# Fixed 256-byte offsets for the split weights of a decoder trunk, and another order of three-product sums

## Chip, cores and metric

The kernel runs on one core of a Trainium2 chip. The metric is the device time of one execution in microseconds; the median of several runs counts.

## What is computed

One layer of a hybrid decoder trunk on 256 tokens of width 1024, in float32. Every large product is an activation (256 tokens) times a weight:

```
proj = rmsnorm(x) @ w_in                      # 1024 x 3088, shared by three head groups
x = x + concat(shortconv, moba attention, gated linear attention) @ w_out
h = rmsnorm(x);  m = rmsnorm(mem)             # mem: 256 tokens
x = x + cross_attention(h @ wq, m @ wkv) @ wo # 4 heads of 64
h = rmsnorm(x)
u = causal_dwconv(h @ w_up)                   # 1024 x 5504, width 3
x = x + (silu(u[:, :2752]) * u[:, 2752:]) @ w_down
return rmsnorm(x)
```

## The kernel before

**Three products for one.** TensorE multiplies float32 data in the type float32r, to which float32 values are rounded. So each operand is split in two: `high` is the value rounded to float32r (a copy on ScalarE, line 159), `low` is the rest (a subtraction on VectorE, line 165). A product is summed in PSUM from (high, high), (high, low) and (low, high); in the code the pairs are (0, 0), (0, 1), (1, 0), the stationary operand first. A tile of 128 output features over 1024 inputs takes 8 blocks of inputs times 3 = 24 matmuls of 256 columns.

**Weights stream in.** `_stream_order` lists all pieces of weights in the order of use, at most 1024 columns each. `emit_load` brings a piece into one of six raw buffers by a DMA on SP's queue; `emit_split` makes its `high` and `low` in two pools of four buffers each (`hp`); `piece` hands them out and keeps six loads and two splits ahead.

**Who is stationary.** In the feature products the weights are the stationary operand and the activations (`xg`, `y`, `xo`, `memg`, `hn2`) move, 256 columns each: `first` (line 300, six output tiles at once), `feature_tile` (line 218: tiles `in`, `xk`, `xq`, `up`), `products` (line 207: `out`), `wo_part` (773) and the first pair of `up` (867). In the token products the activations are stationary and the weights move: `gla` (455, 272 columns), `mv` (471, 512 columns), `memv` (731, 256 columns) and `down` (905 and 909, 512 columns, 260 matmuls at the end of the kernel, with the hidden values `hid` stationary).

**Where the parts lie.** A buffer of `hp` has 1024 + 32 elements, 4224 bytes, which is 16.5 times 256. So the four buffers of a pool begin at 0, 128, 0 and 128 bytes modulo 256 in turn. A weight that moves begins at the buffer's start, a stationary one 16 elements (64 bytes) behind it:

```
at0 = 0 if key[0] in MOVING else ASIDE
hi, lo = (hp.tile([P, SLOT + 32], F32R, tag=tag, ...)[:, at0:at0 + n] for tag in ("high", "low"))
```

**Order.** The instructions of each engine are put in order by the tile framework; VectorE's order in the loop over `first` and some splits are pinned by hand. `feature_tile` lists all (0, 0) products, then all (0, 1), then all (1, 0); blocks in `late` come behind the others.

Of the kernel before, what the change touches and what calls it, by code (L numbers as in the profile page):

```python
# [10 lines left out]
F32 = mybir.dt.float32  # L11
BF16 = mybir.dt.bfloat16
F32R = mybir.dt.float32r
# [6 lines left out]
P = 128  # L20
T = 256
# [21 lines left out]
EARLY, STATS, TURNED = 3, (1, 0), 3  # L43
# [6 lines left out]
SLOT = 1024  # L50


ASIDE = 16
MOVING = ("gla", "mv", "memv", "down", "dtail")

PADDED = 32

# [18 lines left out]
def _width(key):  # L76
    return {"first": 768, "gla": 544}.get(key[0], 1024)
# [3 lines left out]
def trunk(ctx: ExitStack, tc: tile.TileContext, xT, x_rows, w_stream, params, gate, final, out):  # L81
    nc = tc.nc
    pe, act, dve, pool, sp = nc.tensor, nc.scalar, nc.vector, nc.gpsimd, nc.sync

    cp = ctx.enter_context(tc.tile_pool(name="cp", bufs=1))
    rp = ctx.enter_context(tc.tile_pool(name="rp", bufs=RAW))
    hp = ctx.enter_context(tc.tile_pool(name="hp", bufs=PARTS))
# [6 lines left out]
    def ps(name):  # L94
        banks["turn"] += 1
        return pp.tile([P, 512], F32, tag=banks["tags"][banks["turn"] % len(banks["tags"])], name=name)

    def t1(name):
        return t1p.tile([P, T], F32, tag="t1", name=name)

    def t2(name):
        return t2p.tile([P, 2, T], F32, tag="t2", name=name)

    def small(name, n=2):
        return smp.tile([P, 4], F32, tag="sm", name=name)[:, :n]
# [4 lines left out]
    raw, parts = {}, {}  # L110
    spare = {}
# [22 lines left out]
    def emit_split(pin=False):  # L134
        i = state["split"]
        state["split"] += 1
        key = order[i]
        if key[0] == "mem":
            return
        n = _width(key)  # L140
        t = raw[key]
        if key in SPARE:
            tag = SPARE[key]
            if key[-1] == 0:
                spare[tag] = cp.tile([P, 4 * SLOT + 32], F32R, tag=tag, name="spare_" + tag)
            view = lambda c: spare[tag][:, ASIDE + c * SLOT:ASIDE + (c + 1) * SLOT]
            hi, lo = view(2 * key[-1]), view(2 * key[-1] + 1)
        elif key[0] == "dtail":
            hi = cp.tile([P, n], F32R, name="h_dtail")
            lo = lo_dtail  # L150
        else:
            at0 = 0 if key[0] in MOVING else ASIDE
            hi, lo = (hp.tile([P, SLOT + 32], F32R, tag=tag, name=tag[0] + "_" + "_".join(map(str, key)))[:, at0:at0 + n]
                      for tag in ("high", "low"))
        if i == 0:
            act.copy(hi[:, :384], t[:, :384])
            dve.tensor_copy(hi[:, 384:], t[:, 384:n])
        else:
            c = act.copy(hi, t[:, :n])  # L159
            if pin:  # L160
                tc.keep_in_program_order(c)
        if key[0] == "dtail":
            c = dve.tensor_sub(lo[:TAIL], t[:TAIL, :n], hi[:TAIL])
        else:
            c = dve.tensor_sub(lo, t[:, :n], hi)  # L165
        if pin:
            tc.keep_in_program_order(c)
        parts[key] = (hi, lo)

    def piece(*key):  # L170

        i = place[key]
        while state["load"] < min(len(order), i + RAW):
            emit_load()
        while state["split"] < min(len(order), i + 1 + AHEAD, state["until"]):
            emit_split()
        return raw[key] if key[0] == "mem" else parts[key]

    def blocks(w, n):
        return [a.rearrange("p (k n) -> p k n", n=n) for a in w]  # L180
# [9 lines left out]
    def gained(dst, i, src, g, on=act):  # L190

        if on is act:
            act.activation(dst[0][:, i, :], src, AF.Copy, scale=g)  # L193
        else:
            dve.tensor_scalar(dst[0][:, i, :], src, g, None, op0=ALU.mult)
        dve.scalar_tensor_tensor(dst[1][:, i, :], src, g, dst[0][:, i, :], op0=ALU.mult, op1=ALU.subtract)

    def pair(t, n):

        return t[:, 0:n, :], t[:, n:2 * n, :]  # L200
# [5 lines left out]
        for n, (s, m) in enumerate(todo):  # L206
            pe.matmul(dst, s, m, start=(n == 0), stop=(n == len(todo) - 1))  # L207

    def feature_tile(dst, w, src, late=(), at=None, call=None):
        wb = blocks(w, P)  # L210
        ks = [k for k in range(KT) if k not in late]
        term = lambda k: ([a[:, k, :] for a in wb], [a[:, k, :] for a in src])
        todo = [(k, a, b) for g in (ks, late) for a, b in ((0, 0), (0, 1), (1, 0)) for k in g]
        for n, (k, a, b) in enumerate(todo):
            if n == at:
                call()
            s, m = term(k)
            pe.matmul(dst, s[a], m[b], start=(n == 0), stop=(n == len(todo) - 1))  # L218
# [29 lines left out]
    at = cp.tile([P, 4, T], F32, tag="at", name="at")  # L248
# [22 lines left out]
                       channel_multiplier=-1)  # L271
    pool.memset(tri[0:64, 64:128], 0.0)

    rel = cp.tile([P, 384], F32, name="rel")
    pool.iota(rel[:, 0:P], pattern=[[-1, P]], base=0, channel_multiplier=1, allow_small_or_imprecise_dtypes=True)
    pool.iota(rel[:, P:384], pattern=[[-1, T]], base=P, channel_multiplier=1, allow_small_or_imprecise_dtypes=True)
    pool.affine_select(out=rel[:, 0:P], in_=rel[:, 0:P], pattern=[[-1, P]], compare_op=ALU.is_ge, fill=MASKED,
# [15 lines left out]
    with tc.manual_schedule(engines={mybir.EngineType.DVE}):  # L293
        for k in range(KT):
            state["until"] = place[("first", k)] + 1
            gained(xg, k, x[:, k, :], xt[:, k:k + 1], dve)
            w = piece("first", k)
# [23 lines left out]
    def root_of(sums, name):  # L321

        rt = smp.tile([P, 2], F32, tag=name + "_rt", bufs=1, name=name + "_rt")
        act.activation(rt, sums, AF.Ln, bias=eps, scale=1.0 / D)
        act.activation(rt, rt, AF.Exp, scale=-0.5)
        diags = t1(name + "_diag")
        for j in range(2):
            dve.tensor_scalar(diags[:, j * P:(j + 1) * P], ident, rt[:, j:j + 1], float(D), op0=ALU.mult, op1=ALU.mult)
        return rt, diags
# [120 lines left out]
    for i in range(4):  # L450
        w = blocks(piece("gla", i), 272)
# [23 lines left out]
    q = ps("lrT")  # L475
# [72 lines left out]
    for h in range(4):  # L548
        q = ps(f"a{h}")
# [4 lines left out]
    q = ps("keT")  # L554
# [12 lines left out]
    for n, dst in ((0, ue[:, 0:P]), (2, ue[:, P:T]), (1, uo[:, 0:P])):  # L567
        a = 64 * (n % 2)
# [18 lines left out]
    for j in range(2):  # L587
        for h in range(4):
            a = 64 * (h % 2)
# [23 lines left out]
    for c in range(2):  # L613
        g, s = t1(f"g{c}"), t1(f"sg{c}")
# [20 lines left out]
    for i in range(2):  # L635
        q = ps(f"xk{i}")
# [17 lines left out]
    for o in range(KT):  # L654
        q = ps(f"out{o}")
# [46 lines left out]
    for i in range(2):  # L702
        q = ps(f"xq{i}")
# [39 lines left out]
    for c in range(2):  # L743
        o = ps(f"xo{c}")
        for m in range(2):
            for h in (2 * c, 2 * c + 1):
                a = 64 * (h % 2)
# [5 lines left out]
    xg2 = pair(xgt, KT)  # L753
# [5 lines left out]
    def residual_turned(n):  # L759
        for t in range(2):  # L760
            q = acc[t, n] = pp.tile([P, 512], F32, tag="sd", name=f"dn{t}_{n}")
            for k in range(4):
                pe.matmul(q[:, k * P:(k + 1) * P], x2[:, 4 * n + k, t * P:(t + 1) * P], ident, start=(k == 0), stop=(k == 3),
                          is_transpose=True)
            act.activation(t2(f"x2_sq{t}_{n}").rearrange("p a b -> p (a b)"), q, AF.Square,
                           accum_out=sum2[:, 2 * n + t:2 * n + t + 1])
# [30 lines left out]
    hn2 = pair(hnt, KT)  # L797
# [29 lines left out]
    def freed(j, src):  # L827

        s2 = t2(f"us{j}")
        for t in range(2):  # L830
            dve.tensor_mul(s2[:, t, :], src[t], r2)
        return j, [s2[:, 0, :], s2[:, 1, :]]
# [16 lines left out]
    for j in range(NPAIR + 1):  # L849
        tail = j == NPAIR  # L850
        src = []
        for t in range(1 if tail else 2):
            w = piece("uptail") if tail else piece("up", j, t)
            if j > 0:
                q = ps(f"up{j}_{t}")
                src.append(q[:, :T])
                stats = (j, t) == STATS
                feature_tile(q[:, :T], w, xg2 if j < EARLY else hn2, (), 12 if stats else None, second_root)
            elif t == 1:

                q = ps("up0")
                src = [q[:, :T], q[:, T:]]
                for k in range(KT):
                    for tt in range(2):
                        wb = blocks(piece("up", 0, tt), P)
                        for a, b in ((0, 0), (0, 1), (1, 0)):
                            pe.matmul(src[tt], wb[a][:, k, :], xg2[b][:, k, :], start=(k + a + b + tt == 0),
                                      stop=(k == KT - 1 and a == 1 and tt == 1))
                    if k == TURNED:
                        residual_turned(1)  # L870
                tot2 = small("x2_tot")
                dve.tensor_add(tot2, sum2[:, 0:2], sum2[:, 2:4])
                _, diags2 = root_of(tot2, "x2")
                tc.keep_in_program_order(act.preload_act_table_set("silu_and_others"))
            if (j, t) == STATS:
                early.append(freed(*ready.pop()))
                for k in range(0, KT, 2):
                    f = t2(f"hn{k}")
                    dve.tensor_mul(f, x2[:, k:k + 2, :], r2.unsqueeze(1).to_broadcast([P, 2, T]))
                    for i in range(2):  # L880
                        gained(hn2, k + i, f[:, i, :], gain(PG_FFN, k + i))
                activate(*early.pop())
        ready.append((j, src))
        if j >= STATS[0]:
            for args in ready:
                activate(*(freed(*args) if j < EARLY else args))
            ready = []
# [153 lines left out]
```

## Time and profile before

| | |
|---|---|
| median of 3 runs | 331.56 us (331.46 to 331.89) |
| the profiled execution | 332.42 us |
| its span, first to last instruction | 330.7 us |
| TensorE busy | 321.2 us, 97% |
| VectorE busy | 257.3 us, 78% |
| ScalarE busy | 211.0 us, 64% |

The span is what the rows below divide up. Matmuls are pipelined: each lasts longer in the record (some 276 ns for 256 columns) than the time from its start to the next one's start. The rate of a stream of matmuls is therefore read from starts.

### The profile page before, as it was taken

To read this page: it belongs to the slowest core of one execution; us is meant where nothing else is said; L and a number is where in the kernel's file an instruction comes from. 1 tells how busy PE (TensorE), PEld (TensorE's weight loads), DVE (VectorE), ACT (ScalarE), POOL (GpSimd) and SP (SyncE) were. 2 spreads that over 40 slices of the span, in tenths; PEclk is the share of its full clock that TensorE was granted. 3 is DMA by queue.
4 is the path that set the end of the run, shared out by engine and by line. 5 is a ranking of instruction groups with operands and counts; after the bars stand their busy time and mean duration, and the time that the engine had idled before them with its cause. 6 is when DMAs were issued, how large, how long until landed. Compare 5 with 4: busy or idle time off the path is not lost.

```text
span 330.7 us, 6398 instructions
## 1 busy us (share of the span) xinstructions
PE 321.2 (97%) x2462; PEld 296.4 (90%) x2462; DVE 257.3 (78%) x498; ACT 211.0 (64%) x390; POOL 2.7 (1%) x16
## 2 busy tenths in 40 slices
PE   7999999999999999999999999999999999999992
PEld 4899878899999998899999999999999988888881
DVE  6879978797998858588999999898979974444421
ACT  2583999485676647487977676666667753363322
POOL 3000000000000000000000000000000000000000
PEclk9999999999999999999999999999999999999999
DMA  7979862754368643207067877666557766551003
GB/s 216 405 290 311 270 225 93 254 168 154 108 192 298 208 154 127 66 0 251 5 195 231 271 215 229 197 191 192 191 193 203 235 187 208 191 190 65 0 0 127
DMA packets 17888, 60.38 MB, mean 183 GB/s; under 512 B 1969, under 2 KB 2626, under 8 KB 17858
## 3 DMA queue, kind: packets, MB, share of 16 engines
q1 hardware_dynamic: 17426, 59.26, 54.5%
q10 hardware_dynamic: 432, 0.72, 0.6%
q8 instruction: 19, 0.31, 0.4%
q14 instruction: 11, 0.09, 0.1%
HBM read 58.93 MB, written 1.05 MB: 181 GB/s over the span
## 4 chain that ended last, share of the span: by engine, by line
PE 86%; ACT 6%; DVE 4%; DMA 2%; SPq 1%; issue 0%; ACTq 0%
PE up L218 30%; PE dn L905 18%; PE in L218 10%; PE out L207 7%; PE v L471 3%; DMA w_first<-in_w_stream_dram 2%; PE gv L455 2%; PE xv L731 2%; PE wo L773 2%; PE xq L218 2%; PE xk L218 2%; ACT h_up L159 2%; PE first L300 1%; DVE l_first L165 1%; ACT hn L193 1%; PE et L398 1%
## 5 line engine op out<-in xcount | busy, mean ns | idle before, releaser
L218 PE MATMUL up<-hn,h_up 128*128 128x256 f32 x576 | 71.2, 276 | 0.0
L218 PEld LDWEIGHTS up<-hn,h_up 128*128 128x128 f32 x576 | 68.0, 188 | 0.0
L159 ACT CAST h_up<-w_up 128x1024 fp32r<-128x1024 f32 x40 | 41.7, 1049 | 18.9 <-PE up L218 18.9
L905 PE MATMUL dn<-h_down,hid 128*128 128x512 f32 x168 | 52.8, 392 | 0.0
L165 DVE TENSOR_TENSOR l_up<-w_up,h_up 128x1024 fp32r<-128x1024 f32 x40 | 48.7, 1222 | 4.5 <-ACT h_up L159 3.6
L165 DVE TENSOR_TENSOR l_down<-w_down,h_down 128x1024 fp32r<-128x1024 f32 x21 | 25.7, 1224 | 24.5 <-ACT h_down L159 24.5
L218 PE MATMUL up<-hn,l_up 128*128 128x256 f32 x288 | 38.6, 276 | 0.3 <-DVE l_up L165 0.3
L159 ACT CAST h_down<-w_down 128x1024 fp32r<-128x1024 f32 x21 | 22.0, 1047 | 25.7 <-PE dn L905 25.2
L905 PEld LDWEIGHTS dn<-h_down,hid 128*128 128x128 f32 x168 | 31.5, 188 | 7.1
L218 PEld LDWEIGHTS up<-hn,l_up 128*128 128x128 f32 x288 | 35.3, 188 | 0.5 <-DVE l_up L165 0.5
L804 DVE SCALAR_TENSOR_TENSOR u<-up,par,u 128x255 f32<-128x255 f32 (+1 forms) x74 | 34.5, 477 | 0.5
L905 PE MATMUL dn<-l_down,hid 128*128 128x512 f32 x84 | 32.9, 392 | 0.0
L218 PE MATMUL in<-xg,h_in 128*128 128x256 f32 x192 | 25.1, 283 | 0.0
L218 PEld LDWEIGHTS in<-xg,h_in 128*128 128x128 f32 x192 | 23.1, 188 | 0.7 <-issue 0.5
L802 ACT ACTIVATE u<-up,par 128x256 f32<-128x256 f32 x37 | 20.4, 554 | 0.0
L905 PEld LDWEIGHTS dn<-l_down,hid 128*128 128x128 f32 x84 | 15.8, 188 | 3.6
L207 PE MATMUL out<-y,h_out 128*128 128x256 f32 x128 | 16.0, 277 | 0.0
L165 DVE TENSOR_TENSOR l_in<-w_in,h_in 128x1024 fp32r<-128x1024 f32 x12 | 14.5, 1218 | 1.0 <-ACT h_in L159 1.0
L207 PEld LDWEIGHTS out<-y,h_out 128*128 128x128 f32 x128 | 15.3, 188 | 0.0
L159 ACT CAST h_in<-w_in 128x1024 fp32r<-128x1024 f32 x12 | 12.5, 1046 | 4.1 <-issue 2.7
L300 PEld LDWEIGHTS first<-xg,h_first 128*128 128x128 f32 x96 | 11.6, 188 | 3.1 <-ACT h_first L159 2.1
L300 PE MATMUL first<-xg,h_first 128*128 128x256 f32 x96 | 12.8, 282 | 1.6 <-ACT h_first L159 1.4
(270 smaller groups left out, 542.7 us busy)
## 6 DMA issues: line engine op xcount, KB each, us to landing
w_up<-in_w_stream_dram SPq DMA_DIRECT2D x42, 512.0 KB, 4.3
w_down<-in_w_stream_dram SPq DMA_DIRECT2D x21, 512.0 KB, 3.6
w_in<-in_w_stream_dram SPq DMA_DIRECT2D x12, 512.0 KB, 4.6
w_out<-in_w_stream_dram SPq DMA_DIRECT2D x8, 512.0 KB, 3.3
w_first<-in_w_stream_dram SPq DMA_DIRECT2D x7, 384.0 KB, 8.7
w_mv<-in_w_stream_dram SPq DMA_DIRECT2D x4, 512.0 KB, 5.7
w_gla<-in_w_stream_dram SPq DMA_DIRECT2D x4, 272.0 KB, 4.7
xtok<-in_x_rows_dram SPq DMA_DIRECT2D x1, 1024.0 KB, 10.4
```

The lines of the kernel that those rows point to most:

```text
L159: c = act.copy(hi, t[:, :n])
L165: c = dve.tensor_sub(lo, t[:, :n], hi)
L207: pe.matmul(dst, s, m, start=(n == 0), stop=(n == len(todo) - 1))
L218: pe.matmul(dst, s[a], m[b], start=(n == 0), stop=(n == len(todo) - 1))
L300: pe.matmul(fps[i][:, :T], w[a][:, i * P:(i + 1) * P], xg[b][:, k, :], start=(k == 0 and (a, b) == (0, 0)), stop=(k == KT - 1 and a == 1))
L455: pe.matmul(gps[j][:, :272], xg[a][:, 2 * i + k, j * P:(j + 1) * P], w[b][:, k, :], start=(i == 0 and k == 0 and (a, b) == (0, 0)), stop=( ...
L471: pe.matmul(vps[j], xg[a][:, 2 * i + k, j * P:(j + 1) * P], w[b][:, k, :], start=(i == 0 and k == 0 and (a, b) == (0, 0)), stop=(i == 3 an ...
L731: pe.matmul(vps[j][:, :T], mg[a][:, 4 * i + k, j * P:(j + 1) * P], w[b][:, k, :], start=(i == 0 and k == 0 and (a, b) == (0, 0)), stop=(i ...
L773: pe.matmul(wps[o][:, :T], wb[a][:, 2 * (o % 4) + k, :], xo[b][:, k, :], start=(k == 0 and a + b == 0), stop=(k == 1 and a == 1))
L802: act.activation(v, src, AF.Identity, bias=fb(t), scale=fw(t, 2))
L804: dve.scalar_tensor_tensor(v[:, s:], src[:, :T - s], fw(t, 2 - s), v[:, s:], op0=ALU.mult, op1=ALU.add)
L905: pe.matmul(q, hid[i](k)[:, cols], w[j], start=False, stop=(k == NPAIR - 1 and i == 1), skip_group_check=True)
```

## The change

Each buffer of `hp` becomes 1024 + 64 elements, 4352 bytes or 17 times 256, so all buffers begin at 0 modulo 256. Moving weights stay at the start; of stationary weights `high` lies at 64 and `low` at 192. The weights `memv` leave the list of those that lie at the start. The two larger spare tiles, which hold the parts of `wo` and of the first `up` pair, get 32 elements between their quarters. Two paddings (32 elements at `rel` and at the spare tile `parts`) shift what lies behind them by 128 bytes. The scratch that is kept for DMA descriptors shrinks to 4096 bytes and makes room.

The offsets modulo 256, added up from the tiles' sizes in the order of their allocation, in bytes:

| operands | weight before (high / low) | weight after | other operand before | after |
|---|---|---|---|---|
| `first`, `in`, `xq`, `out`: weight stationary | 64 or 192, both alike | 64 / 192 | 128 | 128 |
| `xk`, `up` from the fourth pair on: weight stationary | 64 or 192, both alike | 64 / 192 | 0 | 0 |
| `up`, pairs two and three: weight stationary | 64 or 192, both alike | 64 / 192 | 128 | 128 |
| `up`, first pair: weight stationary | 192 / 192 | 192 / 64 | 128 | 128 |
| `wo`: weight stationary | 192 / 192 | 192 / 64 | 128 | 0 |
| `mv`, `gla`, `down`: weight moves | 0 or 128, both alike | 0 / 0 | 128 | 128 |
| `memv`: weight moves | 0 or 128, both alike | 64 / 192 | 0 | 0 |

In `feature_tile` the second and third products now alternate: after the eight (0, 0) come (0, 1) and (1, 0) of one block, then of the next. So high and low weights take turns as the stationary operand. That holds for 16 tiles (twelve `in`, two `xk`, two `xq`); the `up` tiles keep the old order with `turns=False`. No instruction is added or taken away, and no transfer changes.

```diff
--- before.py
+++ after.py
@@ -51,7 +51,7 @@
 
 
 ASIDE = 16
-MOVING = ("gla", "mv", "memv", "down", "dtail")
+MOVING = ("gla", "mv", "down", "dtail")
 
 PADDED = 32
 
@@ -142,16 +142,16 @@
         if key in SPARE:
             tag = SPARE[key]
             if key[-1] == 0:
-                spare[tag] = cp.tile([P, 4 * SLOT + 32], F32R, tag=tag, name="spare_" + tag)
-            view = lambda c: spare[tag][:, ASIDE + c * SLOT:ASIDE + (c + 1) * SLOT]
+                spare[tag] = cp.tile([P, 4 * (SLOT + 32) + (32 if tag == "parts" else 0)], F32R, tag=tag, name="spare_" + tag)
+            view = lambda c: spare[tag][:, ASIDE + c * (SLOT + 32):ASIDE + c * (SLOT + 32) + SLOT]
             hi, lo = view(2 * key[-1]), view(2 * key[-1] + 1)
         elif key[0] == "dtail":
             hi = cp.tile([P, n], F32R, name="h_dtail")
             lo = lo_dtail
         else:
-            at0 = 0 if key[0] in MOVING else ASIDE
-            hi, lo = (hp.tile([P, SLOT + 32], F32R, tag=tag, name=tag[0] + "_" + "_".join(map(str, key)))[:, at0:at0 + n]
-                      for tag in ("high", "low"))
+            high, low = (0, 0) if key[0] in MOVING else (ASIDE, 3 * ASIDE)
+            hi, lo = (hp.tile([P, SLOT + 64], F32R, tag=tag, name=tag[0] + "_" + "_".join(map(str, key)))[:, at0:at0 + n]
+                      for tag, at0 in (("high", high), ("low", low)))
         if i == 0:
             act.copy(hi[:, :384], t[:, :384])
             dve.tensor_copy(hi[:, 384:], t[:, 384:n])
@@ -206,11 +206,17 @@
         for n, (s, m) in enumerate(todo):
             pe.matmul(dst, s, m, start=(n == 0), stop=(n == len(todo) - 1))
 
-    def feature_tile(dst, w, src, late=(), at=None, call=None):
+    def feature_tile(dst, w, src, late=(), at=None, call=None, turns=True):
         wb = blocks(w, P)
         ks = [k for k in range(KT) if k not in late]
         term = lambda k: ([a[:, k, :] for a in wb], [a[:, k, :] for a in src])
-        todo = [(k, a, b) for g in (ks, late) for a, b in ((0, 0), (0, 1), (1, 0)) for k in g]
+        todo = []
+        for g in (ks, late):
+            todo += [(k, 0, 0) for k in g]
+            if turns:
+                todo += [(k, a, 1 - a) for k in g for a in (0, 1)]
+            else:
+                todo += [(k, a, 1 - a) for a in (0, 1) for k in g]
         for n, (k, a, b) in enumerate(todo):
             if n == at:
                 call()
@@ -271,7 +277,7 @@
                        channel_multiplier=-1)
     pool.memset(tri[0:64, 64:128], 0.0)
 
-    rel = cp.tile([P, 384], F32, name="rel")
+    rel = cp.tile([P, 384 + 32], F32, name="rel")[:, :384]
     pool.iota(rel[:, 0:P], pattern=[[-1, P]], base=0, channel_multiplier=1, allow_small_or_imprecise_dtypes=True)
     pool.iota(rel[:, P:384], pattern=[[-1, T]], base=P, channel_multiplier=1, allow_small_or_imprecise_dtypes=True)
     pool.affine_select(out=rel[:, 0:P], in_=rel[:, 0:P], pattern=[[-1, P]], compare_op=ALU.is_ge, fill=MASKED,
@@ -855,7 +861,7 @@
                 q = ps(f"up{j}_{t}")
                 src.append(q[:, :T])
                 stats = (j, t) == STATS
-                feature_tile(q[:, :T], w, xg2 if j < EARLY else hn2, (), 12 if stats else None, second_root)
+                feature_tile(q[:, :T], w, xg2 if j < EARLY else hn2, (), 12 if stats else None, second_root, turns=False)
             elif t == 1:
 
                 q = ps("up0")
@@ -1026,7 +1032,7 @@
     from concourse import mybir as _mybir
     from concourse.bass_utils import run_bass_kernel_spmd as _run
 
-    nc = _bacc.Bacc("TRN2", target_bir_lowering=False, num_devices=1)
+    nc = _bacc.Bacc("TRN2", target_bir_lowering=False, num_devices=1, dynamic_dma_scratch_size=4096)
     arrays, args = {}, []
     names = ["xT", "x_rows", "w_stream", "params", "gate", "final"]
     for name, a in zip(names, _layout(inputs)):
```

## Rows read from the trace of the kernel before

**Rows 1.** The profile's page: span, and TensorE's busy time, share, instructions.

```profile
span 330.7 us, 6398 instructions
...
PE 321.2 (97%) x2462; PEld 296.4 (90%) x2462; DVE 257.3 (78%) x498; ACT 211.0 (64%) x390; POOL 2.7 (1%) x16
```

**Rows 2.** Waits of TensorE after its start: sum in us, times, longest.

```profile
PE up L218 <- DVE l_up L165: 0.3, 1, 0.3
PE x_r L334 <- DVE x_diag L328: 0.2, 1, 0.2
```

**Rows 3.** The chain that ended last, merged: start us, us, what.

```profile
19.95 4.43 PE first L300 x36
...
144.18 0.45 PE dn L763 x4
...
144.66 1.27 ACT x_sq L765 x4
...
166.04 98.78 PE up L218 x869
```

**Rows 4.** Timeline of TensorE, tiles of `out`: start us, us, instructions merged.

```profile
97.88 2.05 PE L207 MATMUL out<-y,h_out 128*128 128x256 f32 x16
...
103.53 2.05 PE L207 MATMUL out<-y,h_out 128*128 128x256 f32 x16
...
106.36 1.98 PE L207 MATMUL out<-y,h_out 128*128 128x256 f32 x16
...
109.08 1.18 PE L207 MATMUL out<-y,h_out 128*128 128x256 f32 x9
```

**Rows 5.** Timeline of TensorE, three of the twelve `in` tiles.

```profile
24.46 2.23 PE L218 MATMUL in<-xg,h_in 128*128 128x256 f32 x16
...
56.95 2.15 PE L218 MATMUL in<-xg,h_in 128*128 128x256 f32 x16
58.94 1.10 PE L218 MATMUL in<-xg,l_in 128*128 128x256 f32 x8
...
61.41 2.06 PE L218 MATMUL in<-xg,h_in 128*128 128x256 f32 x16
63.31 1.07 PE L218 MATMUL in<-xg,l_in 128*128 128x256 f32 x8
```

**Rows 6.** Timeline of TensorE, first matmul of `down`'s pieces 1 to 4.

```profile
267.37 0.40 PE L905 MATMUL dn<-h_down,hid 128*128 128x512 f32 x1
...
270.17 0.39 PE L905 MATMUL dn<-h_down,hid 128*128 128x512 f32 x1
...
272.90 0.40 PE L905 MATMUL dn<-h_down,hid 128*128 128x512 f32 x1
...
275.69 0.39 PE L905 MATMUL dn<-h_down,hid 128*128 128x512 f32 x1
```

**Rows 7.** Timeline of TensorE, `mv` pieces 0 and 3, second token half.

```profile
39.72 1.10 PE L471 MATMUL v<-h_mv,xg 128*128 128x512 f32 x4
40.65 0.63 PE L471 MATMUL v<-l_mv,xg 128*128 128x512 f32 x2
...
51.41 1.07 PE L471 MATMUL v<-h_mv,xg 128*128 128x512 f32 x4
52.31 0.62 PE L471 MATMUL v<-l_mv,xg 128*128 128x512 f32 x2
```

**Rows 8.** Timeline of TensorE, `wo` and what follows it.

```profile
138.24 5.95 PE L773 MATMUL wo<-xo,spare_big 128*128 128x256 f32 x48
144.02 1.03 PE L763 MATMUL dn<-ident,x 128*128 128x128 f32 x8
```

**Rows 9.** Timeline of TensorE, the first `memv` part.

```profile
127.19 1.11 PE L731 MATMUL xv<-h_memv,memg 128*128 128x256 f32 x8
128.14 0.64 PE L731 MATMUL xv<-l_memv,memg 128*128 128x256 f32 x4
```

**Rows 10.** Timeline of VectorE, the low parts of the first two `in` pieces.

```profile
22.76 2.35 DVE L165 TENSOR_TENSOR l_in<-w_in,h_in 128x1024 fp32r<-128x1024 f32 x2
```

## The prediction

> **What bounds the kernel now.** I read the page first: TensorE is busy for 321.2 us of a span of 330.7 [rows 1], so time can only be won where its matmuls follow each other faster, or where it waits. The list of waits answers the second: after the start it waits for VectorE twice, 0.5 us together [rows 2]. The chain that ended last shows where those waits belong. It enters TensorE at 19.95, leaves it after the four transposes at 144.18 for ScalarE, comes back at 166.04 and then stays to the last product [rows 3]. What TensorE gains from 20 to 144 us and after 166 us shortens the span. What it gains between them (the first three `up` pairs) only lengthens a wait.
>
> So the question is the rate of the matmuls, and the timeline answers it by differences of starts. A tile of `out` is 24 matmuls. Tiles 0 and 1 together take 103.53 - 97.88 = 5.65 us, tile 2 takes 2.83, tile 3 takes 2.72 [rows 4], and so do tiles 4 to 7. That is 117.8 ns a matmul against 113.3, with the same shapes and no wait. Both rates hold for whole tiles and nothing stands between them. I call them the slow and the clean rate. `in` shows both too: behind the same kind of start gap, the 16 products with the high weight take 58.94 - 56.95 = 1.99 us in one tile and 63.31 - 61.41 = 1.90 in another [rows 5].
>
> `down` has its own pattern. Its pieces are 12 matmuls of 512 columns, and their starts lie 2.80, 2.73 and 2.79 us apart [rows 6]: 233.3, 227.5 and 232.5 ns each. Pieces 1, 3, 5 and so on, the slower ones, have their weights at 0 modulo 256 bytes; the even ones at 128. The stationary `hid` is at 128 for all. So here the offset decides the rate, and it does so again and again.
>
> **The slow rate and the offsets.** With weights stationary, offset alone does not decide. A slow tile and a clean one lie at the same offsets (`out` tiles 2 and 4: weight 64, activation 128). What the order of the tiles shows is that a rate persists until something changes the pairing. Within one offset, steady slow streaks of up to 48 matmuls (`wo`, below) never turn clean. Where a slow streak on `xg` or `y` meets a weight buffer at 192 after one at 64, it turns clean within four matmuls, as between `out` tiles 2 and 3; between tiles 0 and 1 it did not. Clean streaks stay clean across the same steps, in both directions: `out` tiles 3 to 7 alternate 192 and 64.
>
> The change brings this step into every tile, since high is now at 64 and low at 192, and in the alternating tiles up to eight times. So I expect slow streaks to end early.
>
> **Part 1, stationary weights: the gain that reaches the end.**
> - `out`: three slow tiles, (5.65 + 2.83) - 3 x 2.72 = 0.32 us [rows 4]. The order stays high, high, low there, so a tile must first run its 16 high products. I take 0.25.
> - `in`: five of the twelve tiles read as slow (the first at 24.46 and the one at 56.95 are shown). The price of one is 0.09 for its 16 high products [rows 5], and half as much for the 8 low ones, some 0.13; a count at 4.5 ns for 24 gives 0.11. Five times 0.11 is 0.55. In the new order a slow start lasts eight high products before the turns begin, a third of the tile, and I take 0.40.
> - `wo`: 48 matmuls between 138.24 and 144.02 [rows 8], less some 0.13 for its start gap, are 117.7 ns each: slow throughout, at weights 192 / 192. At the clean rate 0.21 less; afterwards weights are at 192 / 64, so I take 0.15.
> - `xv` (`memv`): eight products in 128.14 - 127.19 = 0.95 us, 118.8 ns each [rows 9]. Over 48 products the clean rate would give 48 x 5.5 ns = 0.26 us. The new pairing, 64 or 192 against 0, is one that elsewhere shows both rates; I take 0.13.
> - `first` and the two `xq`: one slow block of 18 matmuls after 19.95 and half a tile; 0.14 at most, I take 0.07.
> - The first three `up` pairs, 48 + 24 + 16 slow matmuls or some 0.4 us, fall in the stretch from 144 to 166 that ScalarE and VectorE set [rows 3]. I cost them at nothing: the chain through ScalarE's squares, the diagonal and `l_up` hides them. Were that cover gone, they would give 0.4 more.
>
> The sum is 0.25 + 0.40 + 0.15 + 0.13 + 0.07 = 1.00 us. The bounds are 0 (no streak ends early) and 0.32 + 0.55 + 0.21 + 0.26 + 0.14 = 1.48. A gain beyond the clean rate has no row: 113.3 ns is the lowest steady rate at each offset that the trace shows.
>
> **Part 2, moving weights: the loss.** After the change every piece of `down` begins at 0 and `hid` stays at 128, the pairing of the slower pieces. Eleven of the 21 pieces are at 128 now. Each would go from 2.73 to 2.80 [rows 6]: 11 x 0.07 = 0.77 us; the even pieces' first three matmuls after each change of offset are already slow, so some of it is paid now, and I take 0.70. Bounds: 0, if the slow pairing is a product of the change of offsets from piece to piece and vanishes when all are alike, and 0.77.
>
> `mv` is the same shape. Four products with high weights take 40.65 - 39.72 = 0.93 us at 0 and 52.31 - 51.41 = 0.90 at 128 [rows 7], 7 ns each. 24 of its matmuls go from 128 to 0: 0.17 at most, and as the other pieces differ less, I take 0.10. `gla` has one duration at both offsets, and I cost it at nothing.
>
> **Part 3, the turns.** Low weights are wanted seven matmuls earlier, 7 x 113 ns = 0.8 us. The tightest case is the first `in` tile. VectorE makes its two low parts in 2.35 us from 22.76 [rows 10], so the first is there at about 24.0; the tenth matmul of the tile that begins at 24.46 [rows 5] comes 1.2 us or more later. The other tiles have theirs earlier still. The high buffer is let go 0.8 us later, but its next writer is two pieces on. Nothing is queued behind either: no instruction is added to an engine, SP issues the same transfers, and POOL has none to issue. I cost it at 0; the price if a low part were late is the 0.8 us of one tile.
>
> The sum: -1.00 + 0.70 + 0.10 = -0.20 us on the profiled execution's 332.42. That execution lies 0.86 us above the median of the runs; I take the difference over to the median, 331.56 - 0.2, and predict **331.3 us**. A measurement of this kernel can tell about 0.2%, 0.66 us, from no change.
>
> **A rule against it.** The Trainium skill ("SBUF — State Buffer", section "SBUF: two separate sides") says that within the engine side only the port pair shared by VectorE and GpSimd causes contention, and that TensorE's ports never wait on anyone; "TensorE: Matmul & The Clock Gate", "Step-by-step: what each phase is for", gives TensorE two independent read ports, for the moving and the stationary operand. By that rule the offsets change nothing and the time stays at 331.56. The trace disagrees for `down`, where the rate follows the offset from piece to piece.
>
> **The rivals.**
> - *Down does not pay.* The streaks end as in part 1, and `down`'s slower pairing goes once all pieces are alike: -1.00 to -1.48, so 330.4. For it: the slower pieces are only ever seen 12 matmuls long, between others. Against it: they end at the slower rate rather than drift from it, and `mv` shows the same. Chance 0.27.
> - *The streaks stay, down pays* (the other side of the bound). The turn from 64 to 192 does not end a slow streak; `out` tiles 0 to 1 and 1 to 2 speak for that. Then +0.70 + 0.10 alone, 332.4. It decides as soon as the gain of part 1 is under 0.1. Chance 0.12.
> - *The turns make a rate of their own.* With the stationary offset changing at every matmul, the 16 x 16 = 256 alternating products may settle at the slow rate for good, as the slower `down` pieces settle in theirs. The seven clean `in` tiles, the two `xk` and one and a half `xq` then lose 160 or so x 4.5 ns = 0.7 us, on top of `down`, with the gains of `in` gone: about 332.5. Against it: single steps leave a clean streak clean. Chance 0.07.
> - *Nothing depends on the offset.* The two rates come from how a stream starts, and new starts draw anew: 331.6. For it: `out` tiles 2 and 4 differ at equal offsets. Against it: `down` follows the offset in every piece shown. Chance 0.10.
>
> The forecast has 0.44; its own range is 330.9 to 331.8 (part 1 between 0.6 and 1.3, `down` between 0.5 and 0.77).
>
> **How the numbers follow.** Faster by over 0.2% is below 330.9: most of the first rival, 0.25, and the edge of the forecast, 0.05, so 0.30. Slower is above 332.2: two thirds of the second and third rivals, 0.14. The rest, 0.56, is within. The range goes from the first rival at its lower side, 330.3, to the second at 332.4.
>
> **What would show it.** Right: `out`, `in` and `wo` tiles at 2.72 us per 24 matmuls, with 118 ns only at their beginnings; `down` pieces 2.80 us apart without exception. Wrong: `in` tiles at 118 through their second half; `down` pieces at 2.73 or less; a new wait of `in` for `l_in`; a span changed between 144 and 166 us, if the framework orders ScalarE's and VectorE's work there another way, which I can't read from the diff.

## The result, and the profile after

The changed kernel is slower: median 335.48 us of 15 executions against 331.62 before, ratio 1.0091 (95% interval 1.0069 to 1.0113). The prediction was 331.3, with a range up to 332.4.

The 15 times fall into two groups with nothing between them: eleven from 335.24 to 336.00 and four from 331.43 to 332.32. The kernel before has one group, 331.13 to 331.97. So the change did not make the kernel slower by a fixed amount; it let something happen in most executions. The granted clock does not tell the groups apart: 0.994 to 0.998 of full clock in the eleven, 0.994 or 0.995 in the four. The profiled execution is one of the eleven (335.24 us, span 333.5).

The page of the changed kernel, span and busy times (the two instructions more are semaphore waits; TensorE's 2462 matmuls are the same):

```profile
span 333.5 us, 6400 instructions
...
PE 324.4 (97%) x2462; PEld 299.7 (90%) x2462; DVE 258.2 (77%) x498; ACT 209.9 (63%) x390; POOL 2.7 (1%) x16
```

The chain that ended last, merged, of the same kernel:

```profile
96.96 21.83 PE out L207 x192
...
136.95 5.69 PE wo L779 x48
142.63 0.45 PE dn L769 x4
143.11 1.27 ACT x_sq L771 x4
...
164.47 102.61 PE up L224 x869
267.09 27.88 PE dn L911 x120
```

Against [rows 3], TensorE comes to the transposes 1.55 us earlier (142.63 for 144.18) and to the rest of `up` 1.57 us earlier (164.47 for 166.04). Then the same 869 products of `up` take 102.61 us for 98.78. Those 3.83 us are the whole loss and more. The stretch between the transposes and `up`, which ScalarE and VectorE set, is as long as before: 21.84 for 21.86.

The timeline of TensorE in the changed kernel, from the first `up` tiles that read `hn2`:

```profile
161.74 2.40 PE L224 MATMUL up<-hn,h_up 128*128 128x256 f32 x19
164.47 1.21 PE L224 MATMUL up<-hn,l_up 128*128 128x256 f32 x8 [0.33 <-DVE l_up L165]
165.52 1.69 PE L224 MATMUL up<-hn,h_up 128*128 128x256 f32 x13
167.05 1.10 PE L224 MATMUL up<-hn,l_up 128*128 128x256 f32 x8
168.00 2.04 PE L224 MATMUL up<-hn,h_up 128*128 128x256 f32 x16
169.88 1.10 PE L224 MATMUL up<-hn,l_up 128*128 128x256 f32 x8
170.82 2.04 PE L224 MATMUL up<-hn,h_up 128*128 128x256 f32 x16
...
264.10 2.04 PE L224 MATMUL up<-hn,h_uptail 128*128 128x256 f32 x16
```

A tile is 170.82 - 168.00 = 2.82 us, the slow rate of `out` tiles 0 to 2 in [rows 4], and it stays so to the last tile at 264.10. Sixteen products recorded as 2.04 us are slow, as 1.98 us are clean, so the merged duration alone tells the rate; in [rows 4] the two values are 2.05 and 1.98.

`out` shows the forecast cure. Its first tile starts slow, and everything from its low part on is clean, where before three tiles were slow [rows 4]:

```profile
96.80 2.04 PE L207 MATMUL out<-y,h_out 128*128 128x256 f32 x16
98.68 1.07 PE L207 MATMUL out<-y,l_out 128*128 128x256 f32 x8
99.59 1.98 PE L207 MATMUL out<-y,h_out 128*128 128x256 f32 x16
```

### The profile page after: what moved, and what is told of

Its sections match the earlier page's. It is cut to its first block, busy times and chain, and to the rows that moved or that the text cites. A ratio compares the mean times of both kernels' runs of the same rounds, so it can differ in the third digit from the quotient of the medians.

```text
span 333.5 us, 6400 instructions
## 1 busy us (share of the span) xinstructions
PE 324.4 (97%) x2462; PEld 299.7 (90%) x2462; DVE 258.2 (77%) x498; ACT 209.9 (63%) x390; POOL 2.7 (1%) x16
## 4 chain that ended last, share of the span: by engine, by line
PE 86%; ACT 6%; DMA 4%; DVE 2%; SPq 1%; issue 0%; ACTq 0%
PE up L224 31%; PE dn L911 18%; PE in L224 10%; PE out L207 7%; PE v L477 3%; DMA xtok<-in_x_rows_dram 3%; PE gv L461 2%; PE xv L737 2%; PE xq L224 2%; PE wo L779 2%; PE xk L224 2%; ACT h_up L159 2%; PE first L306 1%; DMA w_first<-in_w_stream_dram 1%; ACT hn L193 1%; PE et L404 1%
## 5 line engine op out<-in xcount | busy, mean ns | idle before, releaser
L224 PE MATMUL up<-hn,h_up 128*128 128x256 f32 x576 | 73.6, 281 | 0.0
L224 PEld LDWEIGHTS up<-hn,h_up 128*128 128x128 f32 x576 | 70.5, 189 | 0.0
L224 PE MATMUL up<-hn,l_up 128*128 128x256 f32 x288 | 39.9, 280 | 0.3 <-DVE l_up L165 0.3
L224 PEld LDWEIGHTS up<-hn,l_up 128*128 128x128 f32 x288 | 36.4, 187 | 0.5 <-DVE l_up L165 0.5
L224 PE MATMUL in<-xg,h_in 128*128 128x256 f32 x192 | 34.5, 283 | 0.0
L224 PEld LDWEIGHTS in<-xg,h_in 128*128 128x128 f32 x192 | 29.2, 188 | 0.7 <-issue 0.3
L224 PE MATMUL in<-xg,l_in 128*128 128x256 f32 x96 | 22.5, 277 | 0.0
L224 PEld LDWEIGHTS in<-xg,l_in 128*128 128x128 f32 x96 | 18.0, 188 | 0.0
```

## The experiments

I count an offset as stationary / moving, modulo 256 bytes. Two theories stood at the start. *Restart*: the stream of `up` starts anew behind its wait for `l_up`, and the offset of the first low weight (192 now, 64 before) decides the rate. *No cure*: the rate of a start is drawn by chance in either kernel, and the kernel before had steps of offset that end a slow streak, while the changed one has none that does. Rivals: the turns are the cause; 64 and 192 against 0 is slow in itself. Each experiment is a change to the changed kernel unless it says otherwise, and medians stand against 331.62 to 331.64 for the kernel before on the same chip.

**e1, the slots without the turns.**

```diff
-    def feature_tile(dst, w, src, late=(), at=None, call=None, turns=True):
+    def feature_tile(dst, w, src, late=(), at=None, call=None, turns=False):
```

> The changed kernel without the turns: the new slots alone. If the slots at the `up` tiles cause the loss (theories restart and no-cure, below), the time is that of the changed kernel, about 335.5 us with some executions near 332, and `in` tiles that start slow stay slow for their 16 high products, some 0.3 us more. If the turns cause the loss (rival), the time falls to 331 to 332 in every execution.

Measured: 335.9 us, all four executions from 335.72 to 336.04; none is near 332, where some were expected. The loss is the slots'. The twelve `in` tiles of its profile, added up from starts, take 35.05 us for 34.62 in the changed kernel, 0.4 more for the 0.3 expected.

**e2, turns in the `up` tiles too, from the sixth pair.**

```diff
-feature_tile(..., second_root, turns=False)
+feature_tile(..., second_root, turns=j > 4)
```

> The changed kernel with the turns in the `up` tiles from the sixth pair on too, where the low parts are ready early. Theory: the `up` stream starts anew behind the wait for `l_up` at 164.5 us, in most executions at the slow rate, and the order high, high, low holds it there; alternating products end a slow streak within a tile as in `in`. Then `up` tiles take 2.72 us from the sixth pair on and every execution lies at 331.4 to 332.4. Rival, the pairing of 64 and 192 against activations at 0 is slow by itself: no change, 335.5 in most executions, or slower.

Measured: 332.29 us, eleven executions from 331.70 to 332.70; ratio 1.0022 (1.0013 to 1.0031). The streak ends, but not as I had thought. In its timeline the first alternating tile (`up` 5, 0) is slower still, 120 ns a product; the streak ends in the eight high products that follow:

```profile
175.25 0.28 PE L224 MATMUL up<-hn,l_up 128*128 128x256 f32 x1
175.37 0.28 PE L224 MATMUL up<-hn,h_up 128*128 128x256 f32 x1
...
176.57 1.20 PE L224 MATMUL up<-hn,h_up 128*128 128x256 f32 x9
...
179.30 1.18 PE L224 MATMUL up<-hn,h_up 128*128 128x256 f32 x9
```

The tile from 176.57 takes 2.73 us. Alternating is no sure cure: it can hold a rate of its own. Four of the eleven executions lie above the 332.4 that was expected of all.

**e3, high at 192 and low at 64 for `up`.**

```diff
+            if key[0] == "up":
+                high, low = 3 * ASIDE, ASIDE
```

> The changed kernel with high at 192 and low at 64 for the `up` pieces alone. Theory restart: the rate is decided by the offset of the first low weight behind the wait (192 after the change, 64 before), so all executions are clean, 331.4 to 332.4. Theory no-cure: the start is drawn by chance at any offset, and only steps of offset can end it; with the same steps in the other direction most or some executions stay at 335.5 and some at 332.

Measured: 331.93 us, ten executions from 331.38 to 332.49; ratio 1.0010 (1.0001 to 1.0019). The median is what *restart* asked for, but the trace shows another way there:

```profile
164.99 1.21 PE L226 MATMUL up<-hn,l_up 128*128 128x256 f32 x8 [0.31 <-DVE l_up L167]
166.04 1.69 PE L226 MATMUL up<-hn,h_up 128*128 128x256 f32 x13
167.57 1.09 PE L226 MATMUL up<-hn,l_up 128*128 128x256 f32 x8
168.49 1.98 PE L226 MATMUL up<-hn,h_up 128*128 128x256 f32 x16
```

The stream starts slow at 64 / 0 as well: 13 high products take 167.57 - 166.04 = 1.53 us, 118 ns each. It turns clean in the low part at 167.57, the step from 192 to 64, behind those 13 products. So *restart* as I had put it falls, and the direction of the step behind the longer run is the point.

**e4 and e6, both parts at 64, or both at 192, for `up`.**

```diff
+            if key[0] == "up":
+                high, low = ASIDE, ASIDE          # e4; 3 * ASIDE twice in e6
```

> The changed kernel with high and low at 64 for the `up` pieces: no step of offset at all from the fourth pair on. Theory restart: the stream starts at 64 as before the change and is clean, 331.4 to 332.4 in every execution. Theory no-cure: executions that start slow have nothing that ends the streak, so a mix of 335.5 and 332 as in the changed kernel.

> The changed kernel with high and low at 192 for the `up` pieces: no step from the fourth pair on. Theory no-cure: a mix again, each execution wholly slow (335.5) or wholly clean (331.5 to 332.4). Theory restart as first put (192 starts slow, 64 clean): all at 335.5. With the run at 64, one of ten was slow, so the share of slow executions here against that one tells how much the offset of the start weighs.

Measured: e4 nine executions from 331.17 to 332.07 and one at 335.56; e6 four executions from 335.00 to 335.76. Without any step an execution is wholly the one or the other. How often an execution is slow does depend on the offset (64: one of ten, 192: four of four), but these runs move the offset of the start and of all that follows together. The profiled e4 shows a slow streak without a step too: its `up` tiles at 64 / 128 run at 2.83 us. Behind the wait at 165 us the tiles, now at 64 / 0, are clean:

```profile
157.10 2.05 PE L226 MATMUL up<-xg,h_up 128*128 128x256 f32 x16
...
159.93 2.05 PE L226 MATMUL up<-xg,h_up 128*128 128x256 f32 x16
...
168.56 1.98 PE L226 MATMUL up<-hn,h_up 128*128 128x256 f32 x16
...
171.28 1.98 PE L226 MATMUL up<-hn,h_up 128*128 128x256 f32 x16
```

**e7, `hn2` at 128.** The refined theory: what ends a slow streak is a step by which the stationary operand, counted from the moving one, goes from 192 to 64. Against 128 that is 64 to 192, the order of the changed kernel; against 0 it is 192 to 64.

```diff
-    hnt = cp.tile([P, 2 * KT, T], F32R, tag="hn", name="hn2")
+    hnt = cp.tile([P, 2 * KT * T + 64], F32R, tag="hn", name="hn2")
+    # hn2 is its elements from 32 on
```

> The changed kernel with the activations hn2 moved from 0 to 128 modulo 256; weights stay at 64 and 192. Theory: what ends a slow streak is a step by which the stationary operand, counted from the moving one, goes from 192 to 64; high (64) to low (192) against 128 is such a step, after 16 high products in every `up` tile. So every execution is clean, 331.4 to 332.4, and a slow streak behind the wait for `l_up` ends at the next tile's low part. Rival, that 64 then 192 is the wrong order for any activation offset: a mix, most at 335.5.

Measured: 331.77 us, eleven executions from 331.53 to 332.26. As in e3 the profiled start is slow (13 high products 165.74 to 167.26) and ends in the next low part:

```profile
165.74 1.69 PE L224 MATMUL up<-hn,h_up 128*128 128x256 f32 x13
167.26 1.09 PE L224 MATMUL up<-hn,l_up 128*128 128x256 f32 x8
168.19 1.98 PE L224 MATMUL up<-hn,h_up 128*128 128x256 f32 x16
```

**e9, the kernel before with its weight buffers shifted by 128 bytes.**

```diff
-            hi = cp.tile([P, n], F32R, name="h_dtail")
+            hi = cp.tile([P, n + 32], F32R, name="h_dtail")[:, :n]
```

> The kernel before with its weight buffers shifted by 128 bytes, so that each stationary weight that lay at 64 lies at 192 and the other way round; the stream of `up` starts anew behind the wait with a low part at 192 against activations at 0, as in the changed kernel. Theory: the start is slow, and the next change from a piece at 192 to one at 64 ends it within one or two tiles, so all executions stay at 331.3 to 332.2. Rival, that a start at 192 decides the rest of `up` in any layout: 335.5.

Measured: 331.57 us, ten executions from 331.03 to 332.11; ratio 1.0001 (0.9992 to 1.0010). The profiled start is slow here too, at the low part of `up` 3, 0 (192 / 0):

```profile
165.82 1.69 PE L218 MATMUL up<-hn,h_up 128*128 128x256 f32 x13
167.35 1.11 PE L218 MATMUL up<-hn,l_up 128*128 128x256 f32 x8
168.30 2.05 PE L218 MATMUL up<-hn,h_up 128*128 128x256 f32 x16
170.18 1.10 PE L218 MATMUL up<-hn,l_up 128*128 128x256 f32 x8
171.12 1.98 PE L218 MATMUL up<-hn,h_up 128*128 128x256 f32 x16
```

The tile from 168.30, a piece at 192, is slow to its end; with the next piece, at 64, the stream is clean. The old slots change the offset from piece to piece, and that is what keeps a slow start from lasting there. The step from 192 to 64 at 165.8, behind only eight products at 192, ended nothing, just as the step from each low part to the next high part ends nothing in the changed kernel.

**e11, one piece of `up` swapped.**

```diff
+            if key == ("up", 8, 0):
+                high, low = 3 * ASIDE, ASIDE
```

> The changed kernel with one single piece of `up`, the first of the ninth pair, swapped to high at 192 and low at 64. Theory: in an execution that starts slow, `up` tiles stay at 2.83 us up to this piece, its step from 192 to 64 ends the streak, and all tiles behind it take 2.72, 26 or so of them: 26 x 0.11 = 2.9 us less, so no execution above 333.3 and a median near 332.6. Rival, that each piece has its own rate by its offsets: the other 39 pieces stay slow, 335.4.

Measured: 332.72 us; six executions from 332.35 to 332.92 and one at 331.79. One piece's offsets, of forty, take 2.8 us from the median. The profiled execution is the one at 331.79, with a clean start, so no trace shows the streak end at this piece; the times alone speak for it. That clean start also answers the rival of the start, that 64 and 192 against 0 is slow in itself: ahead of the swapped piece its `up` tiles lie at these offsets and run clean, a tile here in 171.01 - 168.29 = 2.72 us. The four executions of the changed kernel near 332 ask for the same.

```profile
168.29 1.98 PE L226 MATMUL up<-hn,h_up 128*128 128x256 f32 x16
...
171.01 1.18 PE L226 MATMUL up<-hn,h_up 128*128 128x256 f32 x9
```

**e5, the kernel before with the turns alone.** The new `feature_tile` in the old slots.

> The kernel before with the turns alone, old slots. High and low lie at the same offset there, so taking turns brings no step of offset. Theory (only a step of offset, in one direction, ends a slow streak): no change, 331.4 to 331.9, and the `in` tiles show whole slow tiles as before. Rival, that the order of the products itself ends streaks: `in` tiles clean after their first third, some 0.2 us faster.

Measured: 331.65 us; ratio 1.0003 (0.9994 to 1.0012). Order without a step of offset does nothing to the `in` tiles: the same five are wholly slow.

**e8, `up` swapped, and `mv` and `down` at 128.** For part 2 of the prediction.

```diff
+            if key[0] == "up":
+                high, low = 3 * ASIDE, ASIDE
+            if key[0] in ("mv", "down"):
+                high, low = 2 * ASIDE, 2 * ASIDE
```

> The kernel with `up` swapped (high 192, low 64), and the moving weights of `mv` and `down` at 128 instead of 0. Theory of part 2 of the prediction: 512-column products take 226.7 ns when weight and activation are both at 128, and 233 when the weight is at 0; `down` falls from 60.6 us to 59.0, 1.6 us less than in the swapped kernel, so 330.3 to 330.6 in the median. Rival, that the slower pieces come from the change of offset between pieces: no change against 331.9.

Measured: 330.42 us, from 330.28 to 330.52; ratio 0.9963 (0.9951 to 0.9976), the fastest version here. The chain of e8:

```profile
165.03 98.77 PE up L228 x869
263.81 27.20 PE dn L915 x120
```

`up` has its 98.77 us again, and the first 120 products of `down` take 27.20 us, 226.7 ns each, against 27.88 at 0 (232.3).

**e10, as e8, with the alternating products first.**

```diff
             if turns:
                 todo += [(k, a, 1 - a) for k in g for a in (0, 1)]
+                todo += [(k, 0, 0) for k in g]
```

> The swapped kernel with moving weights at 128, and in the 16 tiles with turns the alternating products come first, the eight high products last. Theory: a slow start of an `in` tile ends within a few products instead of eight to sixteen, so 0.1 to 0.3 us less than without, 330.1 to 330.4. Rival, a slow start ends only behind a run of products at one offset: no gain, 330.4 or a little more.

Measured: 330.82 us, 0.4 more than e8; the forecast gain did not come. Six of its twelve `in` tiles run at 120 ns a product to the end of the alternating products, as this one:

```profile
70.59 0.28 PE L229 MATMUL in<-xg,h_in 128*128 128x256 f32 x1
70.71 0.28 PE L229 MATMUL in<-xg,l_in 128*128 128x256 f32 x1
...
71.55 0.28 PE L229 MATMUL in<-xg,h_in 128*128 128x256 f32 x1
71.67 0.28 PE L229 MATMUL in<-xg,l_in 128*128 128x256 f32 x1
71.79 0.99 PE L229 MATMUL in<-xg,h_in 128*128 128x256 f32 x7
```

## Why the prediction was wrong

**The step that failed.** The prediction said: "Where a slow streak on `xg` or `y` meets a weight buffer at 192 after one at 64, it turns clean", and from it "The change brings this step into every tile ... So I expect slow streaks to end early." It was read at activations at 128 and carried over to every tile. For the `up` tiles on `hn2`, at 0, the sign is the other. There the changed kernel goes from 64 to 192 behind 16 high products, which ended nothing, and from 192 to 64, the step that would cure, only behind eight low ones. And part 1 has no term for the 869 products after 166.04. I had them as clean and took from "Clean streaks stay clean" that they would stay so, although they start anew behind a wait [rows 2, 3]. Their price, 3.83 us, was in no rival. e3, e7, e9 and e11 show the cause from four sides: turn the step round, move the activations, watch the old slots cure a slow start, give one piece the right step (e11 by its times alone). That the rate can change at this wait is seen both ways: the products on `hn2` run at 118 ns ahead of it and at 113 behind it in the kernel before, and in e7 at 113 ahead and 118 behind, the high ones at the same offsets.

**Part 1, the gain.** From the first `in` tile to the transposes TensorE takes 0.5 us less; I had forecast some 0.9 there, 1.00 less the 0.10 of `mv`. `out` gave 0.25, as taken:

```profile
98.04 22.08 PE out L207 x192
...
138.31 5.88 PE wo L773 x48
```

These are the kernel before; the changed kernel has 21.83 and 5.69. So `wo` gave 0.19 of 0.15 forecast, but that is luck and not the slots' doing. Its 48 products run clean in e5, with the old slots:

```profile
137.99 5.68 PE wo L779 x48
```

They run slow in e1, with the new ones:

```profile
137.44 5.93 PE wo L779 x48
```

Over all profiles `wo` is clean in two of three with the old slots and in five of ten with the new. `in` gave 0.10 of 0.40: seven tiles start slow in the changed kernel where five were slow before, and the streaks end after 9 to 19 of the 24 products. `xv` gave 0.05 of 0.13; it stays at 117 to 118 ns. That the first `up` pairs gain nothing was right: the wait for the diagonal grew from 0.2 to 0.4 us and the stretch kept its length. The first stage ends some 1.0 us earlier, which I do not attribute: its end lies between 23.2 and 24.2 us in the profiled executions of all these kernels, the old slots among them (23.5 to 24.2).

**Part 2, the loss.** The 252 products of `down` on full pieces take 60.19 us from first to last start for 59.65 before: 0.53, before rounding, for the 0.70 forecast, and 0.07 in `mv` for 0.10. The rival "down does not pay" is refuted, and e8 shows the same pairing from the other side: 58.77 us at 128.

**Part 3.** No wait for `l_in` appeared, and e5 shows that the turns cost nothing in the old slots.

**The rivals.** "The turns make a rate of their own" got 0.07 and concerned the right kind of danger: e2 and e10 show such a rate. It was not what happened here. "Nothing depends on the offset" is out by e3 and e11; its other half, that new starts draw anew, was the nearest that any rival came to what happened. With the same instructions and another offset of one operand, e8's `down` is 1.4 us shorter than the changed kernel's (58.77 us for 60.19). The rule of the Trainium skill that stands beside this rival ("SBUF — State Buffer", "SBUF: two separate sides": TensorE's ports never wait on anyone), read as the prediction read it, that offsets change nothing, does not agree with that.

With `up` cured, the changed kernel would be at 331.93 (e3) or 331.77 (e7), against my 331.3: the sum without the failed step was off by half a microsecond, mostly the gain of part 1, which was some 0.6 of the 1.00, with `wo`'s 0.19 by luck. Two slips of the working change nothing: 331.56 - 0.2 is 331.4 and not 331.3, and two thirds of the second and third rivals are 0.13 and not 0.14.

**What stays open.** Why a streak keeps its rate, why the ends seen are steps in the one direction, and how long the run ahead of the step must be, no run here shows; these are rules read from the traces, and they have exceptions. Between `out` tiles 0 and 1 of the kernel before, the step in the right direction ended nothing behind 24 products (the prediction names it), and in three `in` tiles of e1 it ended nothing behind 16. On the other side, two of the seven slow `in` tiles of the changed kernel turn clean at this step behind only nine, as here, where the rate changes at 56.98 us:

```profile
55.81 1.33 PE L224 MATMUL in<-xg,h_in 128*128 128x256 f32 x9
56.98 0.28 PE L224 MATMUL in<-xg,l_in 128*128 128x256 f32 x1
```

The other five turn clean among the alternating products. The share of slow starts is from few executions each. The times do not tell how many executions of e3 and e7 started slow and were cured; one profile of each shows it, while e8 and e10, with e3's slots for `up`, start clean in theirs.

## What to carry to other kernels

Read the rate of a matmul stream from starts, tile by tile, before costing it: where one shape shows two rates, ask of every long stretch, clean ones too, what put it at its rate and what would bring it back. A stretch that restarts behind a wait is a stretch whose rate may be drawn anew, and the largest such stretch sets the risk, not the ones that a change is aimed at. Run such a kernel more than three times: the first three executions of the changed kernel gave 335.24, 335.92 and 331.43.

## What the runs showed of the hardware

- 256-column float32r products behind weight loads run at 113.3 or 117.8 ns each with equal instructions, and can keep the rate for 100 us and more (the 869 products of `up`: 102.61 us in the changed kernel, 98.78 before).
- A slow streak can end where the stationary operand's offset, counted from the moving one's modulo 256 bytes, goes from 192 to 64: in e3 and e7 it did behind 13 products at 192, in e9 behind 24. It does not at every such step (`out` tiles 0 to 1 before, three `in` tiles of e1). Behind eight products it ended nothing in the `up` tiles of the profiled changed kernel; behind nine it did in two of its `in` tiles.
- Offsets that alternate at every product can hold a third rate, 120 ns a product in the mean (e2, e10).
- 512-column products run at 226.7 ns with weight and activation both at 128 modulo 256, and at 232 to 233 with the weight at 0 (e8, the changed kernel).
